# 4-MB weight units, another order of an expert's work, and the scatter as two float32r products

## The chip, the cores and the metric

One core of a Trainium2 chip runs the whole layer. The metric is the device time of one execution in microseconds (us), the median of several runs. The engines are named as the profile names them: PE is TensorE, PEld its weight loads, DVE VectorE, ACT ScalarE, POOL GpSimd, SP SyncE, which here only issues DMAs. Each engine works through its own list of instructions in the order in which the list stands.

## The reference

One post-norm decoder layer in float32 on 256 tokens of 1024 features: a mixer (a state-space branch and a gated-MLP branch), cross-attention into 256 memory tokens, and a mixture of 32 experts of which each token takes 4. The change lies in the experts:

```python
def expert_step(acc, p):
    wgu, bgu, wd, bd, g = p
    hgu = xt @ wgu + bgu
    gate = jnp.minimum(hgu[:, :D_EXPERT], SWIGLU_LIMIT)
    up = jnp.clip(hgu[:, D_EXPERT:], -SWIGLU_LIMIT, SWIGLU_LIMIT)
    glu = gate * jax.nn.sigmoid(SWIGLU_ALPHA * gate)
    y = ((up + 1.0) * glu) @ wd + bd
    return acc + g[:, None] * y.astype(f32), None
```

`g` holds a token's four softmax gates and zeros for the other experts. An expert's `w_gu` is 1024 x 2048 (8 MB), its `w_down` 1024 x 1024 (4 MB), so the experts read 384 MB, each byte once.

## The kernel before

**Phase A** (layer norm, mixer, attention, router) ends at about 392 us. It is not touched but for the names of some buffers. Towards its end SP already loads the first 22 MB of expert weights, in 1-MB pieces, into buffers that phase A leaves (`FIRST`).

**The experts** follow, two at a time as a pair (`Pair`). For a pair a 0/1 matrix picks at most 64 tokens per expert. For one expert:

- gather: products of the tokens with the 0/1 matrix (`gather`, L971), the result scaled on ACT and DVE;
- gate and up: 8 steps k of `products(k)` (L1037), each four products that stream 512 columns of weights, and then four bias products (L1044);
- SwiGLU on DVE and ACT, `gc`, `sg`, `uc` (L1049 to L1053), each instruction behind the one before;
- `hidden_t`: four transposes of `uc` on PE (L1062) and a copy on ACT (`hT`, L1063);
- down: 16 products (L1076) into `y`, which both experts of a pair share;
- after the odd expert the scatter (L1079 to L1092): ACT copies `y` to `ys` in three pieces, PE multiplies `ys` by `PT`, the transposed 0/1 matrix times the gates, in four float32 products, and DVE adds the four results to `acc`.

A float32 product of 512 columns shows as two rows in the trace, a float32r product as one. The list of PE is made by a scheduler from the order in which the program is written, and its result can differ from that order. In the program the first `AHEAD` = 2 steps of the next expert are written between the bias products and the transposes of this one.

**The weights** come in one DMA queue, issued by SP in the order of use. After `FIRST` they go round a ring of 20 MB of buffers, as ten units of 2 MB (`RING`); a unit can be issued once PE has read what lay in its place. `PT` of the next pair is made between the gathers (`weights`, L984). In expert 16 `add_rest` adds the residual and the bias of `w_down` (`b_down`, loaded in two DMAs into buffers that it shares with `ys`); it has small products with operands of 32 rows (`norm_row`, L937).

**The end**: the last pair has a form of its own. Expert 31 does its gate and up before expert 30's down; expert 30's down comes as 1-MB pieces, and expert 31's down as four column pieces of 1 MB (`w_last`), each with its own products, ACT and DVE steps and scatter (`down_piece`, `scatter_piece`).

Of the kernel before, what the change touches and what calls it, by code (L numbers as in the profile page):

```python
# [8 lines left out]
F32 = mybir.dt.float32  # L9
# [40 lines left out]
def block_kernel(ctx: ExitStack, tc: tile.TileContext, a, out):  # L50
# [12 lines left out]
    arena = cp.tile([P, len(SLOTS), 2048], F32, name="arena")  # L63
    big = ctx.enter_context(tc.tile_pool(name="big", bufs=1))

    def two(tag, dt=F32):

        return big.tile([P, 2, 2048], dt, tag=tag, name=uniq(tag))

# [133 lines left out]
    def w_parts():  # L203
        t = two(("t01", "t23")[tcount[0] % 2], F32R).rearrange("p q (i c) -> p q i c", i=2)
        tcount[0] += 1
        return [[t[:, q, i] for q in range(2)] for i in range(2)]
# [155 lines left out]
    keys(2, wk2)  # L362
    xh, xl = feat("xhl")
    for k2 in range(4):
# [330 lines left out]
    proj_residual(hh, hl, x0, x1, st)  # L695
    xh, xl = feat("xhl")
    bg3 = bgs[:96, :].bitcast(BF16)
# [255 lines left out]
    class Pair:  # L953
# [39 lines left out]
    def expert_w(src, apart=False):  # L993

        i = ucount[0]
        ucount[0] += 1
        if 2 * i < len(FIRST):
            t = []
            for h in range(2):
                name = FIRST[2 * i + h]  # L1000
                with tc.issue_after(wload[PHASE_A.index(FIRST_AFTER.get(name, ("wo", 3)))].ins):
                    if name in SLOTS:
                        t.append(bt(name))
                    elif name == "d":
                        t.append(cd[:, 1])
                    else:
                        if h == 0:
                            both = two(name)
                        t.append(both[:, h])
                    nc.sync.dma_start(t[h], src[:, h])  # L1010
            return t
        name = RING[(i - len(FIRST) // 2) % len(RING)]
        if name in SLOTS:
            at = SLOTS.index(name)
            t = arena[:, at:at + 2, :]
        else:
            t = two(name)
        if apart:
            for h in range(2):
                nc.sync.dma_start(t[:, h], src[:, h])  # L1020
        else:
            nc.sync.dma_start(t, src)
        return [t[:, h] for h in range(2)]
# [41 lines left out]

    def down(src, odd, hT, y, apart=False, between=None):

        for u in range(2):
            if u and between is not None:
                between()  # L1070
            w = expert_w(src(u), apart)
            for b in range(4):
                k = 4 * u + b
                for n in range(2):
                    o = 64 * (n ^ odd)
                    te.matmul(y[n][o:o + 64, :], hT[:, b, 64 * u:64 * u + 64],  # L1076
                              w[b // 2][:, b % 2 * D + n * 512:b % 2 * D + (n + 1) * 512], start=(k == 0), stop=(k == KB - 1))

    def scatter(y, PT, first=False):  # L1079
        ys = [wk.tile([P, 512], F32, tag="ux", name=uniq("ys")) for n in range(2)]  # L1080
        se.activation(ys[0], y[0], AF.Copy)  # L1081
        se.activation(ys[1][0:64, :], y[1][64:128, :], AF.Copy)
        se.activation(ys[1][64:128, :], y[1][0:64, :], AF.Copy)
        for n in range(2):
            for c in range(2):
                ps = pst("sm", 2)
                te.matmul(ps, PT[:, c, :], ys[n], start=True, stop=True)  # L1087
                av = acc[:, c, n * 512:(n + 1) * 512]
                if first:
# [44 lines left out]

    AHEAD = 2
    st = stats_tile(4)
# [4 lines left out]
    def before(e, k):  # L1141
# [12 lines left out]
        if e % 2 and k == 5:  # L1154
            p.weights()

    def begin(e):
        xg = pairs[e // 2].xg
        current[e] = gate_up(lambda u: a["w_gu"][e, u], i96[:, e:e + 1], lambda k: xg[:, k, e % 2 * CAP:(e % 2 + 1) * CAP],
                             lambda k: before(e, k), e == NE - 1)  # L1160

    begin(0)
    for k in range(AHEAD):
        current[0][0](k)
    for e in range(NE - 2):
# [23 lines left out]
    for k in range(AHEAD, KB):  # L1189
        current[ea][0](k)  # L1190
    uc = current[ea][1]()
    begin(eb)
    for k in range(AHEAD):
        current[eb][0](k)
    hT = hidden_t(uc)
    for k in range(AHEAD, KB):
# [8 lines left out]
    PT = pairs[ea // 2].PT  # L1205
    for q in range(4):
        if q % 2 == 0:
            w = expert_w(a["w_last"][q // 2], True)
        down_piece(hTb[0], w[q % 2], q, ys)
        if q:  # L1210
# [6 lines left out]
    with tc.For_i(0, nx, 1):  # L1217
# [35 lines left out]
        hT = hidden_t(swiglu())  # L1253
        down(lambda u: a["w_down"][bass.ds(ev, 1), u].rearrange("e p h d -> p (e h) d"), 0, hT, y)
        ys = wk.tile([P, 512], F32, tag="ux", name="ysx")
# [11 lines left out]
        for i in range(2):  # L1267
# [8 lines left out]

FIRST = ["e1", "k", "g", "gb", "xhl", "xhl", "w3", "w4", "e0", "x0", "ab", "ab", "w5", "w0", "w1", "w2", "t01", "t01", "t23",
         "t23", "j", "d"]
SLOTS = ["e1", "k", "g", "gb", "w3", "w4", "e0", "x0", "w5", "w0", "w1", "w2", "j", "h"]
FIRST_AFTER = {"e1": ("z", 1), "k": ("wq", 0), "g": ("wq", 1), "gb": ("wo", 0)}  # L1280

RING = FIRST[0:20:2]

# [15 lines left out]
def arrange(inputs):  # L1299
# [56 lines left out]
```

## Time and profile before

| | us |
|---|---|
| median of 3 runs (lowest, highest) | 1319.06 (1317.76, 1319.45) |
| the profiled execution | 1316.82 |
| its span (first to last instruction) | 1315.1 |
| phase A | 0 to 391.85 |
| experts, to the first column piece of `w_last` | 391.85 to 1288.5 |
| column pieces, last norm, output | 1288.5 to 1315.1 |

Over the span PE is busy 95%, DVE 34%, ACT 24%. The mean granted clock of PE is 0.988 of full speed. 464.4 MB of weights and inputs went through SP's queue. The profile's idle time of an engine is put down to what ended it; idle time of an engine that nobody waits for costs nothing.

### The profile page before, as it was taken

How to read it: one execution, taken by the hardware profiler on the slowest of the kernel's cores; microseconds unless marked ns; L12 is line 12 of the kernel's file. 1: busy time of each engine (PE TensorE's matmuls, PEld its weight loads, DVE VectorE, ACT ScalarE, POOL GpSimd, SP SyncE). 2: the span in 40 equal slices, each digit the busy share in tenths (PEclk: the TensorE clock that was granted, in tenths of full speed). 3: DMA queues.
4: the chain of work that ended last, by engine and by line, in shares of the span. 5: the costliest groups of instructions: out<-in, count | busy, mean ns of one | idle time of the engine just before them, and what ended most of it. 6: DMA issues, size and time to landing. Idle time of an engine off the chain costs nothing.

```text
span 1315.1 us, 15885 instructions
## 1 busy us (share of the span) xinstructions
PE 1250.8 (95%) x6757; PEld 684.9 (52%) x6758; DVE 450.3 (34%) x791; ACT 315.5 (24%) x536; POOL 29.1 (2%) x49
## 2 busy tenths in 40 slices
PE   6999999999999999999999999999999999989895
PEld 6899899989873443343333433333343433323232
DVE  4569766687441212121221112232221212212124
ACT  4746665444531111111111111101110111101000
POOL 2110000001000000000000000000000000000000
PEclk9999999999999999999999999969999999999998
DMA  9655543586788999999999999999999999999993
GB/s 357 239 176 196 192 161 133 184 290 227 275 322 353 425 426 427 427 427 428 429 428 427 428 428 427 412 428 427 427 428 428 427 428 427 428 427 427 428 424 160
DMA packets 43930, 472.00 MB, mean 359 GB/s; under 512 B 5104, under 2 KB 6928, under 8 KB 10064
## 3 DMA queue, kind: packets, MB, share of 16 engines
q1 hardware_dynamic: 39840, 464.41, 85.9%
q10 hardware_dynamic: 4016, 6.55, 1.6%
q8 instruction: 54, 0.88, 0.3%
q14 instruction: 20, 0.16, 0.0%
HBM read 469.49 MB, written 1.05 MB: 358 GB/s over the span
## 4 chain that ended last, share of the span: by engine, by line
PE 75%; DMA 18%; DVE 3%; ACT 2%; issue 1%; POOL 1%; ACTq 0%; DVEq 0%; SPq 0%; POOLq 0%
PE gu L1037 25%; PE y L1076 14%; DMA t<-in_w_gu_dram 6%; PE mm L255 6%; PE mm L239 5%; PE mm L238 5%; PE mm L237 5%; PE sm L971 4%; PE sm L1087 3%; DMA arena<-in_w_down_dram 3%; DMA ab<-in_w_gu_dram 3%; DMA arena<-in_w_gu_dram 3%; DMA t<-in_w_down_dram 2%; PE sm L1062 1%; DVE t L181 1%
## 5 line engine op out<-in xcount | busy, mean ns | idle before, releaser
L1037 PE MATMUL gu<-arena,cd 128*64 128x512 f32 x1240 | 279.8, 594 | 4.8 <-DMA arena<-in_w_gu_dram 4.8
L1037 PEld LDWEIGHTS gu<-arena,cd 128*64 128x64 f32 x1240 | 86.6, 137 | 171.5 <-issue 157.1
L181 DVE TENSOR_TENSOR t<-arena,t 128x1024 fp32r<-128x1024 f32 (+1 forms) x111 | 131.9, 1210 | 49.6 <-ACT t L180 49.6
L1076 PE MATMUL y<-arena,hT 128*64 128x512 f32 x592 | 140.7, 616 | 6.8 <-ACT hT L1063 5.6
L180 ACT ACTIVATE t<-arena 128x1024 fp32r<-128x1024 f32 (+1 forms) x114 | 113.8, 1038 | 59.2 <-PE mm L255 19.1
L1049 DVE TENSOR_SCALAR gc<-gu 128x512 f32<-128x512 f32 x32 | 22.1, 692 | 297.9 <-PE gu L1044 297.9
L237 PE MATMUL mm<-xhl,t 128*128 128x256 f32 x384 | 110.5, 288 | 0.0
L239 PE MATMUL mm<-xhl,t 128*128 128x256 f32 x384 | 108.8, 283 | 1.7 <-DVE t L181 1.7
L238 PE MATMUL mm<-xhl,t 128*128 128x256 f32 x384 | 108.7, 283 | 0.0
L1050 ACT ACTIVATE sg<-gc 128x512 f32<-128x512 f32 x32 | 20.2, 630 | 342.1 <-DVE gc L1049 342.1
L975 DVE TENSOR_SCALAR cd<-sm,par 128x128 f32<-128x128 f32 x64 | 26.2, 410 | 210.7 <-ACT cd L973 210.5
L1092 DVE TENSOR_TENSOR cd<-sm,cd 128x512 f32<-128x512 f32 x56 | 38.7, 692 | 169.3 <-PE sm L1087 169.3
L1076 PEld LDWEIGHTS y<-arena,hT 128*64 128x64 f32 x592 | 42.6, 140 | 85.9 <-issue 74.7
L1037 PE MATMUL gu<-t,cd 128*64 128x512 f32 x384 | 87.1, 595 | 0.1
L973 ACT ACTIVATE cd<-sm,par 128x128 f32<-128x128 f32 x64 | 29.3, 457 | 227.4 <-PE sm L971 226.0
L971 PEld LDWEIGHTS sm<-pair,arena 128*128 128x128 f32 x512 | 62.0, 191 | 31.7 <-issue 27.2
L239 PEld LDWEIGHTS mm<-xhl,t 128*128 128x128 f32 x384 | 73.5, 191 | 1.9 <-DVE t L181 1.9
L971 PE MATMUL sm<-pair,arena 128*128 128x128 f32 x512 | 71.3, 285 | 3.2 <-ACT pair L989 1.8
L238 PEld LDWEIGHTS mm<-xhl,t 128*128 128x128 f32 x384 | 73.6, 192 | 0.2
L237 PEld LDWEIGHTS mm<-xhl,t 128*128 128x128 f32 x384 | 73.5, 191 | 0.2
L1087 PE MATMUL sm<-ys,pair 128*128 128x512 f32 x120 | 59.1, 615 | 10.4 <-ACT ys L1081 10.2
L1037 PEld LDWEIGHTS gu<-t,cd 128*64 128x64 f32 x384 | 26.5, 137 | 50.3 <-issue 48.3
(314 smaller groups left out, 1447.8 us busy)
## 6 DMA issues: line engine op xcount, KB each, us to landing
arena<-in_w_gu_dram SPq DMA_DIRECT2D x71, 2048.0 KB, 31.8
arena<-in_w_down_dram SPq DMA_DIRECT2D x35, 2048.0 KB, 30.0
arena<-in_wa_dram SPq DMA_DIRECT2D x56, 1024.0 KB, 5.1
t<-in_w_gu_dram SPq DMA_DIRECT2D x22, 2048.0 KB, 33.8
ab<-in_w_gu_dram SPq DMA_DIRECT2D x13, 2048.0 KB, 30.1
xhl<-in_w_gu_dram SPq DMA_DIRECT2D x12, 2048.0 KB, 29.5
t<-in_w_down_dram SPq DMA_DIRECT2D x12, 2048.0 KB, 30.9
arena<-in_w_gu_dram SPq DMA_DIRECT2D x13, 1024.0 KB, 7.3
```

Of the source, the lines that this page charges most:

```text
L180: se.activation(h, src, AF.Copy)
L181: sub_op[0] = (eng or ve).tensor_tensor(l, src, h.bitcast(F32), ALU.subtract)
L237: te.matmul(ps[:, b, :], wh, xh[:, k, :], start=(k == 0), stop=False)
L238: te.matmul(ps[:, b, :], wh, xl[:, k, :], start=False, stop=False)
L239: te.matmul(ps[:, b, :], wl, xh[:, k, :], start=False, stop=(k == KB - 1))
L255: last[0] = te.matmul(res[c], x[:, k, c * P:(c + 1) * P], w[k // 2 % 2][:, k % 2, :], start=(k == 0 and i == 0), stop=(k == KB - 1 and i = ...
L971: te.matmul(pg[:, b, :], x2[:, c, k * P:(k + 1) * P], self.t[:, 0, c, :], start=(c == 0), stop=(c == 1))
L973: se.activation(self.xg[:, k, :], pg[:, 0, :], AF.Identity, bias=b2[:, k:k + 1], scale=g2[:, k:k + 1])
L1037: te.matmul(t[64 * j:64 * j + 64, :], xe(k), ws[k][:, n * D + j * 512:n * D + (j + 1) * 512], start=(k == 0), stop=False)
L1076: te.matmul(y[n][o:o + 64, :], hT[:, b, 64 * u:64 * u + 64], w[b // 2][:, b % 2 * D + n * 512:b % 2 * D + (n + 1) * 512], start=(k == 0), ...
L1087: te.matmul(ps, PT[:, c, :], ys[n], start=True, stop=True)
L1092: ve.tensor_tensor(av, ps, av, ALU.add)
```

## The change

- **Units.** The weights are laid out in HBM so that half of `w_gu` (4 MB), or the whole of `w_down`, is one block. The ring is five groups of four 1-MB slots (`RING = [8, 0, 12, 4, 16]`). Experts 0 to 3 still load in units of 2 MB, later ones in 4 MB; the last half of expert 31's `w_gu` and expert 30's `w_down` in units of 2 MB, `w_last` in 1 MB as before. Former pairs of buffers (`xhl`, `ab`, `t01`, `t23`) are now parts of two tiles of four slots.
- **Order.** `AHEAD` is 4. Written order: steps 4 to 7 of this expert, bias, SwiGLU, steps 0 to 2 of the next expert, transposes, step 3, down.
- **Scatter**, all pairs but the last. ACT's copy that makes `PT` also sums each row, which is the gate of that slot; DVE compares `PT` with 0 and gets a 0/1 matrix in float32r (`to`). ACT makes `hs`, the gated `ys` rounded to float32r, and DVE `ls`, the gated `ys` less `hs`. Eight float32r products (`to` with `hs` and with `ls`) take the place of four float32 ones. They are written behind the first steps of the next expert (`go`, called in `finish_products`).
- **`b_down`** is one DMA into a free slot (`j`) that nothing else uses by then.

The diff, cut to its core:

```diff
-RING = FIRST[0:20:2]
+RING = [8, 0, 12, 4, 16]
+NRING = 4 * len(RING)
...
-        bd = [wk.tile([NE, 512], F32, tag="ux", name=uniq("bd")) for n in range(2)]
-        for n in range(2):
-            nc.sync.dma_start(bd[n], a["b_down"][:, n * 512:(n + 1) * 512])
+        t = bt("j")
+        nc.sync.dma_start(t[:NE, :D], a["b_down"])
+        bd = [t[:NE, n * 512:(n + 1) * 512] for n in range(2)]
...
-            se.activation(self.PT, pt, AF.Copy)
+            if self.p == NE // 2 - 1:
+                se.activation(self.PT, pt, AF.Copy)
+                return
+            self.gates = wk.tile([P, 2], F32, tag="smx", name=uniq("gt"))
+            se.activation(self.PT, pt, AF.Copy, accum_out=self.gates[:, 0:1])
+            self.to = [wk.tile([P, P], F32R, tag="cbm", name=uniq("to")) for c in range(2)]
+            for c in range(2):
+                ve.tensor_scalar(self.to[c], self.PT[:, c, :], 0.0, None, op0=ALU.is_gt)
...
-            if k % 2 == 0:
-                ws[k], ws[k + 1] = expert_w(src(k // 2), last and k == KB - 2)
+            if k % 4 == 0:
+                ws.update(enumerate(expert_w(src(k // 4), n_rows[k // 4]), k))
...
-    def scatter(y, PT, first=False):
+    def scatter(y, pair, first):
+
         ys = [wk.tile([P, 512], F32, tag="ux", name=uniq("ys")) for n in range(2)]
         se.activation(ys[0], y[0], AF.Copy)
+        se.activation(ys[1][64:128, :], y[1][0:64, :], AF.Copy)
         se.activation(ys[1][0:64, :], y[1][64:128, :], AF.Copy)
-        se.activation(ys[1][64:128, :], y[1][0:64, :], AF.Copy)
+
+        hs, ls = ([wk.tile([P, 512], F32R, tag=t, name=uniq("s" + t)) for n in range(2)] for t in ("lm", "t2"))
+        g = pair.gates[:, 0:1]
         for n in range(2):
-            for c in range(2):
-                ps = pst("sm", 2)
-                te.matmul(ps, PT[:, c, :], ys[n], start=True, stop=True)
...
+            se.activation(hs[n], ys[n], AF.Copy, scale=g)
+            ve.scalar_tensor_tensor(ls[n], ys[n], g, hs[n].bitcast(F32), ALU.mult, ALU.subtract)
+
+        def go():
+            for n in range(2):
+                for c in range(2):
+                    ps = pst("sm", 2)
+                    te.matmul(ps, pair.to[c], hs[n], start=True, stop=False)
+                    te.matmul(ps, pair.to[c], ls[n], start=False, stop=True)
...
+        return go
...
-    AHEAD = 2
+    AHEAD = 4
...
+    def rows_of(e):
+
+        return (2, 2) if e < 4 else (4, 4)
...
+    def finish_products(e):
+
         products, swiglu = current.pop(e)
         for k in range(AHEAD, KB):
             products(k)
-        uc = swiglu()
+            if ready:
+                ready.pop()()
+        return swiglu()
+
+    for e in range(NE - 2):
+        uc = finish_products(e)
         begin(e + 1)
-        for k in range(AHEAD):
+        for k in range(AHEAD - 1):
             current[e + 1][0](k)
         hT = hidden_t(uc)
+        current[e + 1][0](AHEAD - 1)
...
-        down(lambda u: a["w_down"][e, u], b, hT, y)
+        down(a["w_down"][e], b, hT, y, rows_of(e)[0])
...
-            scatter(y, pairs.pop(e // 2).PT, e == 1)
+            ready.append(scatter(y, pairs.pop(e // 2), e == 1))
...
-    down(lambda u: a["w_down"][ea, u], 0, hT, y, True, lambda: hTb.append(hidden_t(uc)))
+    down(a["w_down"][ea], 0, hT, y, 2, lambda: hTb.append(hidden_t(uc)))
```

What the scheduler makes of it is read from the lists of the two programs.

PE before, from the last bias product of the odd expert 11 (`gu_4949`) to its first down product; `gu_5062` and `gu_5063` are the gate and up of expert 12:

```order
L1044 LDWEIGHTS i_109
L1044 MATMUL gu_4949<-bgs,i_109 64x512
L1037 MATMUL gu_5062<-t_35_5064,cd_3791 64x512 x2
L1037 MATMUL gu_5063<-t_35_5064,cd_3791 64x512 x2
L1037 MATMUL gu_5062<-t_35_5064,cd_3791 64x512 x2
L1037 MATMUL gu_5063<-t_35_5064,cd_3791 64x512 x2
L1062 MATMUL sm_5075<-ident,uc_5056 128x128 x4
L1076 MATMUL y_6_4973<-arena,hT_5074 64x512
```

PE of the changed kernel at the same place (`gu_4931` is expert 11's up, `gu_5044` and `gu_5045` expert 12's gate and up):

```order
L1063 LDWEIGHTS i_109
L1063 MATMUL gu_4931<-bgs,i_109 64x512
L1081 MATMUL sm_5060<-ident,uc_5038 128x128 x4
L1056 MATMUL gu_5044<-arena,cd_3731 64x512 x2
L1056 MATMUL gu_5045<-arena,cd_3731 64x512 x2
```

The next expert's products stood between the bias and the transposes, two steps of them, and now stand behind the transposes, four steps, ahead of down. It is so for the odd experts from 5 to 29 and for 4 and 30, 15 in all. For the 12 even experts from 6 to 28, eight gather products stand between bias and transposes, and on DVE the scaling of the first gather's result (a 128x128 instruction) stands ahead of `uc`'s last step. Experts 0 to 3 still have 12 products of the next expert there.

PE before at the end of expert 11's down, the last two down products and the scatter:

```order
L1076 MATMUL y_6_4973<-arena,hT_5074 64x512
L1076 MATMUL y_6_4974<-arena,hT_5074 64x512
L1087 MATMUL sm_5104<-ys_5099,pair_4708 128x512
L1087 MATMUL sm_5107<-ys_5099,pair_4708 128x512
L1087 MATMUL sm_5110<-ys_5100,pair_4708 128x512
L1087 MATMUL sm_5113<-ys_5100,pair_4708 128x512
L1037 MATMUL gu_5062<-xhl_5116,cd_3791 64x512 x2
```

PE of the changed kernel there; `slm` is `hs`, `st` is `ls`:

```order
L1093 MATMUL y_6_4970<-arena,hT_5059 64x512
L1093 MATMUL y_6_4971<-arena,hT_5059 64x512
L1113 MATMUL sm_5105<-slm_5092,to_5009 128x512
L1113 MATMUL sm_5109<-slm_5092,to_5010 128x512
L1114 MATMUL sm_5105<-st_11_5094,to_5009 128x512
L1114 MATMUL sm_5109<-st_11_5094,to_5010 128x512
L1113 MATMUL sm_5113<-slm_5093,to_5009 128x512
L1114 MATMUL sm_5113<-st_12_5095,to_5009 128x512
L1056 MATMUL gu_5044<-four_2_3788,cd_3731 64x512 x2
L1056 MATMUL gu_5045<-four_2_3788,cd_3731 64x512 x2
L1113 MATMUL sm_5117<-slm_5093,to_5010 128x512
L1114 MATMUL sm_5117<-st_12_5095,to_5010 128x512
```

Written behind step 4 of the next expert, six of the eight products stand right behind down, as the four before did. It is so for 14 pairs; in the first pair they stand among expert 2's products.

DVE of the changed kernel at this place (`uc_5038` is expert 11's; `sm_5105` to `sm_5117` are the scatter's results):

```order
L1072 SCALAR_TENSOR_TENSOR uc_5038<-uc_5038,gc_5036 128x512
L1107 SCALAR_TENSOR_TENSOR st_11_5094<-ys_5087,gt_5007,slm_5092 128x512
L1119 TENSOR_TENSOR cd_3731<-sm_5105,cd_3731 128x512
L1107 SCALAR_TENSOR_TENSOR st_12_5095<-ys_5088,gt_5007,slm_5093 128x512
L1119 TENSOR_TENSOR cd_3731<-sm_5109,cd_3731 128x512
L1119 TENSOR_TENSOR cd_3731<-sm_5113,cd_3731 128x512
L1119 TENSOR_TENSOR cd_3731<-sm_5117,cd_3731 128x512
```

Before, the four adds stood there alone; the second `ls` now stands behind the first add. On ACT the order is now: first `ys`, first `hs`, the two pieces of the second `ys`, second `hs`.

## Rows read from the trace of the kernel before

**Rows 1.** Windows: us, busy us per engine (PE, PEld, DVE, ACT, POOL), clock, DMA

```profile
391.85:1099.00 707.15, 687.17 (x3241) 267.89 (x3243) 146.08 (x295) 85.27 (x160) 0.00 (x0) 0.99 1.00 423
1099.00:1288.50 189.50, 173.11 (x806) 61.99 (x802) 33.39 (x60) 19.61 (x36) 0.00 (x0) 1.00 1.01 427
```

**Rows 2.** Waits of PE from 391.85 to 1288.5: in total, times, longest

```profile
PE sm L1087 <- ACT ys L1081: 10.2, 15, 0.7
PE y L1076 <- ACT hT L1063: 9.8, 14, 0.7
PE gu L1037 <- DMA arena<-in_w_gu_dram: 4.8, 6, 1.2
...
PE sm L1062 <- DVE uc L1053: 0.9, 1, 0.9
...
PE y L1076 <- DMA ab<-in_w_down_dram: 0.2, 1, 0.2
```

**Rows 3.** Timeline of PE, experts 2 and 3; start, us, [idle before it]

```profile
454.00 3.22 PE L1037 MATMUL gu<-xhl,cd 128*64 128x512 f32 x13
...
491.25 0.60 PE L1044 MATMUL gu<-bgs,i 96*64 96x512 bf16 x4
491.68 3.60 PE L1037 MATMUL gu<-arena,cd 128*64 128x512 f32 x16
495.22 0.66 PE L1062 MATMUL sm<-ident,uc 128*128 128x128 f32 x4
496.56 3.65 PE L1076 MATMUL y<-xhl,hT 128*64 128x512 f32 x16 [0.69 <-ACT hT L1063]
...
504.33 3.96 PE L1087 MATMUL sm<-ys,pair 128*128 128x512 f32 x8 [0.68 <-ACT ys L1081]
508.21 1.08 PE L1037 MATMUL gu<-arena,cd 128*64 128x512 f32 x4
```

**Rows 4.** Timeline of expert 31's bias products, SwiGLU and transposes

```profile
1277.75 0.60 PE L1044 MATMUL gu<-bgs,i 96*64 96x512 bf16 x4
...
1278.18 0.69 DVE L1049 TENSOR_SCALAR gc<-gu 128x512 f32<-128x512 f32 x1 [14.53 <-PE gu L1044]
...
1278.97 0.63 ACT L1050 ACTIVATE sg<-gc 128x512 f32<-128x512 f32 x1 [12.73 <-DVE gc L1049]
...
1279.63 0.69 DVE L1052 TENSOR_TENSOR gc<-gc,sg 128x512 f32<-128x512 f32 x1 [0.16 <-ACT sg L1050]
1280.36 0.69 DVE L1053 SCALAR_TENSOR_TENSOR uc<-uc,gc 128x512 f32<-128x512 f32 x1
...
1281.19 0.63 PE L1062 MATMUL sm<-ident,uc 128*128 128x128 f32 x4 [0.88 <-DVE uc L1053]
```

**Rows 5.** Timeline of a scatter: last down products and copies on ACT

```profile
657.99 7.09 PE L1076 MATMUL y<-t,hT 128*64 128x512 f32 x32 [0.69 <-ACT hT L1063]
...
665.11 0.60 ACT L1081 ACTIVATE ys<-y 128x512 f32<-128x512 f32 x1 [7.17 <-PE y L1076]
665.73 0.59 ACT L1082 ACTIVATE ys<-y 64x512 f32<-64x512 f32 x1
...
666.34 0.59 ACT L1083 ACTIVATE ys<-y 64x512 f32<-64x512 f32 x1
```

**Rows 6.** Groups of lines on PE, 300 to 391.85: busy, mean ns

```profile
L255 PE MATMUL mm<-t,cd 128*128 128x512 f32 x96 | 23.0, 395 | 0.3 <-DVE t L181 0.3
```

**Rows 7.** Groups of lines, 391.85 to 1288.5: gather products, scaling on DVE

```profile
L971 PE MATMUL sm<-pair,arena 128*128 128x128 f32 x512 | 71.3, 285 | 3.2 <-ACT pair L989 1.8 <-DVE pair L963 0.7 <-ACT hT L1063 0.6
...
L975 DVE TENSOR_SCALAR cd<-sm,par 128x128 f32<-128x128 f32 x64 | 26.2, 410 | 210.7 <-ACT cd L973 210.5
```

**Rows 8.** Windows behind `add_rest`'s small products

```profile
852.00:856.00 4.00, 2.94 (x21) 2.18 (x19) 2.78 (x7) 0.60 (x1) 0.00 (x0) 1.00 0.99 422
860.00:876.00 16.00, 16.00 (x40) 6.07 (x38) 5.40 (x9) 0.00 (x0) 0.00 (x0) 0.50 1.01 425
```

**Rows 9.** Window of 1-MB loads

```profile
1268.00:1288.00 20.00, 17.19 (x80) 5.26 (x76) 2.97 (x5) 1.48 (x3) 0.00 (x0) 1.00 1.01 420
```

More of the change, by code (lines that the diff above doesn't have):

```diff
@@ L64, in block_kernel, with fours @@
     big = ctx.enter_context(tc.tile_pool(name="big", bufs=1))
+    four = {}
+    def fours(i, dt):
+        if (i, dt) not in four:
+            four[i, dt] = big.tile([P, 4, 2048], dt, tag=f"four{i}", name=uniq(f"four{i}"))
+        return four[i, dt]
     def two(tag, dt=F32):
-        return big.tile([P, 2, 2048], dt, tag=tag, name=uniq(tag))
+        if tag == "cd":
+            return big.tile([P, 2, 2048], dt, tag=tag, name=uniq(tag))
+        at = SLOTS_R.index(tag)
+        return fours(at // 4, dt)[:, at % 4:at % 4 + 2, :]
     def bt(tag, shape=(P, 2048)):
@@ L203, in w_parts @@
     def w_parts():
-        t = two(("t01", "t23")[tcount[0] % 2], F32R).rearrange("p q (i c) -> p q i c", i=2)
+        t = two(("t0", "t2")[tcount[0] % 2], F32R).rearrange("p q (i c) -> p q i c", i=2)
         tcount[0] += 1
@@ L362, in block_kernel @@
     keys(2, wk2)
-    xh, xl = feat("xhl")
+    xh, xl = feat("xh")
     for k2 in range(4):
@@ L384, in block_kernel @@
     gbm = bt("g").rearrange("p (g d) -> p g d", g=2)
-    gvu = two("ab")
-    gv = gvu[:, 0].rearrange("p (c d) -> p c d", c=2)
+    gv = bt("h").rearrange("p (c d) -> p c d", c=2)
     st = stats_tile(2)
@@ L988, in weights @@
                 te.transpose(pt[:, c, :], G[:, c].rearrange("p b s -> p (b s)"), ident)
-            se.activation(self.PT, pt, AF.Copy)
-    ucount = [0]
[L993 to L1023, printed above, removed]
@@ new lines, in block_kernel, with slots, expert_w @@
+    ucount = [0]
+    rcount = [0]
+    def slots(i, n):
+        if i < len(SLOTS_R):
+            return fours(i // 4, F32)[:, i % 4:i % 4 + n, :]
+        i -= len(SLOTS_R)
+        return arena[:, i:i + n, :]
+    def expert_w(src, n=1):
+        out = []
+        h = src.shape[1]
+        while len(out) < h:
+            i = ucount[0]
+            if i < len(FIRST):
+                m, name = 1, FIRST[i]
+                if name == "d":
+                    t = cd[:, 1:2]
+                else:
+                    t = slots((SLOTS_R + SLOTS).index(name), 1)
+                after = tc.issue_after(wload[PHASE_A.index(FIRST_AFTER.get(name, ("wo", 3)))].ins)
+            else:
+                m = min(n, h - len(out))
+                at = (rcount[0] + NRING - len(FIRST) % 4) % NRING
+                assert at % m == 0
+                rcount[0] += m
+                t = slots(RING[at // 4] + at % 4, m)
+                after = ExitStack()
+            ucount[0] += m
+            with after:
+                nc.sync.dma_start(t, src[:, len(out):len(out) + m])
+            out += [t[:, q] for q in range(m)]
+        return out
@@ L1027, in gate_up @@
+    def gate_up(src, sel, xe, before=None, n_rows=(4, 4)):
         gp, up = pst("gu", 4), pst("gu", 4)
@@ L1064, in hidden_t, with down @@
         return hT
-    def down(src, odd, hT, y, apart=False, between=None):
-        for u in range(2):
-            if u and between is not None:
+    def down(src, odd, hT, y, rows=4, between=None):
+        w = expert_w(src, rows)
+        for k in range(KB):
+            if k == 4 and between is not None:
                 between()
[L1071 to L1077, printed above, removed]
@@ L1079, in scatter @@
-    def scatter(y, PT, first=False):
+            for n in range(2):
+                o = 64 * (n ^ odd)
+                te.matmul(y[n][o:o + 64, :], hT[:, k % 4, 64 * (k // 4):64 * (k // 4) + 64],
+                          w[k // 2][:, k % 2 * D + n * 512:k % 2 * D + (n + 1) * 512], start=(k == 0), stop=(k == KB - 1))
+    def scatter(y, pair, first):
         ys = [wk.tile([P, 512], F32, tag="ux", name=uniq("ys")) for n in range(2)]
         se.activation(ys[0], y[0], AF.Copy)
+        se.activation(ys[1][64:128, :], y[1][0:64, :], AF.Copy)
@@ new lines, in go @@
+        def go():
+            for n in range(2):
+                for c in range(2):
+                    ps = pst("sm", 2)
+                    te.matmul(ps, pair.to[c], hs[n], start=True, stop=False)
+                    te.matmul(ps, pair.to[c], ls[n], start=False, stop=True)
+                    av = acc[:, c, n * 512:(n + 1) * 512]
+                    if first:
+                        ve.tensor_copy(av, ps)
+                    else:
+                        ve.tensor_tensor(av, ps, av, ALU.add)
@@ L1159, in begin @@
         current[e] = gate_up(lambda u: a["w_gu"][e, u], i96[:, e:e + 1], lambda k: xg[:, k, e % 2 * CAP:(e % 2 + 1) * CAP],
-                             lambda k: before(e, k), e == NE - 1)
+                             lambda k: before(e, k), (4, 2) if e == NE - 1 else rows_of(e))
     begin(0)
@@ L1164, in block_kernel @@
         current[0][0](k)
-    for e in range(NE - 2):
+    ready = []
+    def finish_products(e):
         products, swiglu = current.pop(e)
@@ L1186, in block_kernel @@
                 acc = cd[:, 1].rearrange("p (c d) -> p c d", c=2)
-            scatter(y, pairs.pop(e // 2).PT, e == 1)
+            ready.append(scatter(y, pairs.pop(e // 2), e == 1))
     ea, eb = NE - 2, NE - 1
-    for k in range(AHEAD, KB):
-        current[ea][0](k)
-    uc = current[ea][1]()
+    uc = finish_products(ea)
     begin(eb)
-    for k in range(AHEAD):
+    for k in range(AHEAD - 1):
         current[eb][0](k)
     hT = hidden_t(uc)
-    for k in range(AHEAD, KB):
+    for k in range(AHEAD - 1, KB):
         current[eb][0](k)
@@ L1205, in block_kernel @@
     PT = pairs[ea // 2].PT
+    w = expert_w(a["w_last"])
     for q in range(4):
-        if q % 2 == 0:
-            w = expert_w(a["w_last"][q // 2], True)
-        down_piece(hTb[0], w[q % 2], q, ys)
+        down_piece(hTb[0], w[q], q, ys)
         if q:
@@ L1253, in block_kernel @@
         hT = hidden_t(swiglu())
-        down(lambda u: a["w_down"][bass.ds(ev, 1), u].rearrange("e p h d -> p (e h) d"), 0, hT, y)
+        down(a["w_down"][bass.ds(ev, 1)].rearrange("e p h d -> p (e h) d"), 0, hT, y)
         ys = wk.tile([P, 512], F32, tag="ux", name="ysx")
@@ L1330, in arrange @@
     wg, wd = I["w_gu"][0], I["w_down"][0]
-    r["w_gu"] = wg.reshape(NE, 4, 2, P, 2 * D).transpose(0, 1, 3, 2, 4)
-    r["w_down"] = wd.reshape(NE, 2, 4, P, D).transpose(0, 1, 3, 2, 4).reshape(NE, 2, P, 2, 2 * D)
-    r["w_last"] = wd[NE - 1].reshape(KB, P, 4, 256).transpose(2, 1, 0, 3).reshape(2, 2, P, 2 * D).transpose(0, 2, 1, 3)
+    r["w_gu"] = wg.reshape(NE, 2, 4, P, 2 * D).transpose(0, 1, 3, 2, 4)
+    r["w_down"] = wd.reshape(NE, KB, P, D).transpose(0, 2, 1, 3).reshape(NE, P, 4, 2 * D)
+    r["w_last"] = wd[NE - 1].reshape(KB, P, 4, 256).transpose(1, 2, 0, 3).reshape(P, 4, 2 * D)
     r["b_gu"], r["b_down"] = I["b_gu"][0], I["b_down"][0]
```

22 lines of the change are left out of this document (8 added, 14 removed).

## The prediction

> **What bounds the kernel now.** I read the windows of the expert phase first, then PE's waits, then the timelines of PE, DVE and ACT where the change reorders them. The windows show two kinds of bound at once [rows 1]. The DMA engines are busy throughout (last columns: share 1.00 and 1.01, 423 and 427 GB/s). PE is busy too: up to 1099 us it is idle for 707.15 - 687.17 = 20.0 us, behind that for 189.50 - 173.11 = 16.4 us. The reader is to see how the 36.4 us divide. PE's waits for a DMA are five rows, 4.8 us the longest and 0.2 us the last, 10.4 us in sum [rows 2], and they lie behind 1099. Before that nothing on PE waits for weights; it waits for ACT, 10.2 us at the scatter and 9.8 us at down. So PE sets the pace for most of the phase: it enters it behind, with 22 MB of weights already there, and the transfers run ahead by up to the ring's 20 MB. A pair of experts takes PE 508.21 - 454.00 = 54.2 us [rows 3], its 25.17 MB take the DMA engines 25.17 / 0.427 = 58.9 us. PE gains 4.7 us in a pair, and only after some twelve pairs has it caught up. The kernel is within 10.4 us of being bound by PE alone, so what PE gets to wait for or to do beyond that is paid in full, while a faster transfer is paid only as long as PE can follow.
>
> **The change, part by part.** All terms are PE's time from 391.85 to 1288.5 us. It is an account that closes: busy time plus named waits.
>
> *Transposes behind the bias.* Before, the transposes stood behind two steps of the next expert and began without a wait: bias at 491.25, products at 491.68, transposes at 495.22 with nothing idle ahead of them [rows 3]. Now they follow the bias at once in 15 experts. How long SwiGLU takes shows where it was nearly uncovered, at expert 31: the bias products end at 1277.75 + 0.60 = 1278.35, then come 0.69 us on DVE, 0.63 on ACT, 0.69 and 0.69 on DVE, and the transposes start at 1281.19 [rows 4]. That is 2.84 us, and 15 x 2.84 = 42.6. In the 12 even experts eight gather products, sixteen rows of the trace, cover 16 x 71.3 / 512 = 2.2 us of it [rows 7], but one scaling of 0.41 us now stands ahead of `uc`'s last step on DVE: 2.84 + 0.41 - 2.23 = 1.02, and 12 x 1.02 = 12.2. Together +54.8 us. From below, without that scaling's delay, 12 x 0.61, so 50; from above 55 and a little, as each restart of PE costs something. What is queued behind the waiting transposes is the whole of PE's list, and with it the release of the ring's slots. What goes: down now has four steps of products between it and its transposes, so its wait for `hT` (0.69 in the row of 496.56) is covered, -9.8; expert 31's transposes come behind eight down products, 3.5 us, -0.9.
>
> *Scatter.* Work: four float32 products take 508.21 - 504.33 = 3.88 us [rows 3]. A float32r product of 512 columns takes 23.0 / 96 = 0.24 us in phase A [rows 6], eight take 1.92. 15 x 1.96 = -29.4. Waits: the old one was for the first copy of `y`, 0.68 us each, -10.2 in all [rows 2]. The new chain from down's end at 657.99 + 7.09 = 665.08: first `ys` ready at +0.63 (665.11 + 0.60) [rows 5], first `hs`, a copy of the same size on the same engine, at +1.25, first product at +1.30, wait 1.30. Two products, 0.48; first `ls` on DVE (0.69, as `uc`'s last step of the same shape) ready at +2.03, wait 0.25. Two products to +2.51; ACT meanwhile does the two pieces of `ys` (0.59 each) and the second `hs`, ready at +3.13, wait 0.62. One product; the second `ls` stands on DVE behind the first add and is ready at +3.88, wait 0.51. The last two products stand behind four others and wait for nothing. That is 2.7 us in a pair; in the 14 pairs where they stand so, +37.5. Nearest rows from both sides: 1.25 us, which two ACT copies in a row need at least, 14 x 1.25 = 17.5; and up to 3.2 us, if the adds get in the way more often, 45. I take 37.5, since each link of the chain has a row.
>
> *Units of 4 MB.* 1-MB loads run at 420 GB/s [rows 9], 2-MB ones at 427: 2 x 2.497 - 4.911 = 0.08 us that a load costs beside its bytes. 84 pairs of loads become one, 84 x 0.083 = -7.0 us of DMA time. It is worth the 10.4 us of PE's waits at most, and with PE later than the transfers those go anyway: -10.4. No row has 4-MB loads. At the 420 GB/s of the 1-MB ones a unit would take 9.99 us rather than 9.82, and the 81 of them 14 us more in all: the transfers would still end ahead of a PE that ends 32 us later, so the term stays; at any faster rate it stays too. SP's order of loads is the old one (second half of `w_gu`, first half of the next, `w_down`), but a unit now needs four slots free instead of two. It is issued up to two steps later, some 3.5 us [rows 3], and the ring's lead covers that.
>
> *Without cost.* `b_down` no longer waits for the buffers of `ys`; only SP waited, and nothing on PE behind it. The added work on DVE and ACT (two `ls`, two `hs`, two comparisons a pair) falls on engines that were busy 146 and 85 of 707 us [rows 1]; where they are on PE's path it is counted above. The last down unit of expert 30 is 2 MB and lands as one, which leaves four more products behind its landing; with all weights there in time this is nothing, else 1.8 us. Phase A keeps its products; a few us either way belong to the range.
>
> *Sum:* 54.8 - 9.8 - 0.9 + 37.5 - 10.2 - 29.4 - 10.4 = +31.6. On the profiled execution's 1316.82 (span 1315.1) that is 1348.4. The median of the runs is 2.2 above it, so 1351. By the lower bounds, 50 - 10.7 + 17.5 - 10.2 - 29.4 - 14 (DMA waits, if each also cost a slow restart) = +3; by the upper ones, 56 and 45, +40. That is 1322 to 1359.
>
> *PE's clock.* The granted clock fell once in the phase. In 852 to 856 PE was busy 2.94 of 4 us, with products on 32 rows, and behind that, 860 to 876, the clock was 0.50, the lower level (1.2 GHz), though PE never paused [rows 8]. Those 16 us cost 8, about 10 with the edges (my estimate). I keep this fall in the sum, since `add_rest`'s products remain. The Trainium skill ("TensorE: Matmul & The Clock Gate", section "HAM oscillation — how this bites in real kernels") speaks against the change: idle gaps between groups of products let the clock fall, and each return is paid anew. By it the 2.84 us gaps might bring falls of their own, the third rival; by the row alone, where no gap was that long, there are none.
>
> **The rivals.**
>
> 1. *The transfers stay the bound, so PE's waits cost nothing.* The end of the phase goes by the DMA queue, full at 427 GB/s; PE would need 54.2 - 1.4 - 2.0 + 2.8 + 1.0 + 2.7 = 57.3 us for a pair, still under 58.9. Then the merged loads' -7.0 and the last unit's +1.8 give -5.2: 1311.6, 1314 as a median. For it: both numbers, and that PE waited for weights at the end. Against: PE gains only 1.6 us in a pair instead of 4.7, over 14 pairs 22 instead of 66, and it needed twelve pairs at 4.7 to catch up. It decides once the new waits are under 92.3 - 31.6 - 5.2 = 55 us rather than 92. At 61 there is no change.
> 2. *No clock fall at `add_rest`.* Its small products stand between others now. -10: 1341, still slower. Against: the same products, and nearly as close.
> 3. *More falls of the clock*, behind waits of 2.8 us, where PE does less in 4 us than it did in 852 to 856. +10 for each: 1361 with one, 1381 with three. Against: those products had 32 rows, the new gaps lie between full ones.
> 4. *The scatter's chain is mostly covered*, only its first two copies being seen: 17.5 instead of 37.5, so +11.6, 1331. Against: six of the eight products stand ahead of any other work of PE.
>
> **How the numbers follow.** My forecast 1351 (own range 1341 to 1360) 0.52; rival 1 0.13, at 1314; rival 2 0.15; rival 3 0.12; rival 4 0.08. The likeliest gives 1351. From below, rival 1 is left out (0.13), and from above rival 3 with two or more falls (0.06): 1320 to 1373. Within 0.2%, 2.6 us, counts as the same, which is about what a measurement of this kernel tells from no change. Rival 1 is faster but for its upper edge (0.12 and 0.01); the lower edges of rivals 4 and 2 may be the same (0.04); the rest is slower: faster 0.12, same 0.05, slower 0.83.
>
> **What would show it.** PE waits for DVE's `uc` at the transposes: 27 times, 55 us in sum, 2.8 the longest. At the scatter PE waits for ACT and DVE, some 37 us in sum. Its waits for a DMA are gone, and SP waits for PE to the end of the ring. Eight scatter products take 1.9 us. The transfers end over 10 us ahead of the first column piece, which begins near 1320. The forecast is wrong if PE still waits for weights behind 1200, if the transposes' waits are under 2 us, or if the clock takes part otherwise than once, behind `add_rest`.

## The result, and the profile after

| | before | changed |
|---|---|---|
| median, us (lowest, highest) | 1319.15 (1317.76, 1319.45), 4 runs | 1376.52 (1376.06, 1378.82), 4 runs |
| the profiled execution, its span | 1316.82, 1315.1 | 1378.82, 1377.1 |
| ratio to before | | 1.0445, 95% interval 1.0433 to 1.0458 |
| mean granted clock | 0.988 | 0.964 |

The change makes the kernel slower, as forecast, but by 57 us instead of 32, and outside the range. The chain that ended last holds no DMA any more, where it was 18% before:

```profile
PE 87%; DVE 8%; ACT 3%; issue 1%; DMA 0%; ACTq 0%; DVEq 0%
```

The waits of PE in the expert phase, 387 to 1345 us (in total, times, longest), against [rows 2]:

```profile
PE sm L1081 <- DVE uc L1072: 52.9, 27, 2.8
PE sm L1113 <- ACT slm L1106: 20.2, 14, 1.4
PE sm L1113 <- DVE cd L1119: 9.0, 14, 0.6
```

No wait for a DMA is left, and none for `hT`. The wait at the transposes is there 27 times, as counted from the order. The timeline of expert 11 shows one of the 15 long ones, from the bias products to the next expert's first ones (start, us, engine, what; idle before it in brackets), against [rows 3, 4]:

```profile
724.51 0.60 PE L1063 MATMUL gu<-bgs,i 96*64 96x512 bf16 x4
...
724.94 0.69 DVE L1068 TENSOR_SCALAR gc<-gu 128x512 f32<-128x512 f32 x1 [13.20 <-PE gu L1063]
...
725.72 0.63 ACT L1069 ACTIVATE sg<-gc 128x512 f32<-128x512 f32 x1 [14.43 <-DVE gc L1068]
726.38 0.69 DVE L1071 TENSOR_TENSOR gc<-gc,sg 128x512 f32<-128x512 f32 x1 [0.16 <-ACT sg L1069]
727.11 0.69 DVE L1072 SCALAR_TENSOR_TENSOR uc<-uc,gc 128x512 f32<-128x512 f32 x1
...
727.86 1.11 PE L1081 MATMUL sm<-ident,uc 128*128 128x128 f32 x4 [2.74 <-DVE uc L1072]
...
728.90 8.11 PE L1056 MATMUL gu<-arena,cd 128*64 128x512 f32 x32
```

The reader is to see two things. The chain of DVE and ACT is the one of expert 31 before, and PE idles 2.74 us for it. And the four transposes take 1.11 us, where they took 0.63 [rows 4]. The windows tell why (us, busy us of PE, PEld, DVE, ACT, POOL, clock, DMA share, GB/s), against [rows 1, 8]:

```profile
387.20:1353.80 966.60, 875.80 (x4045) 336.65 (x4045) 202.62 (x415) 127.42 (x241) 0.00 (x0) 0.95 0.94 396
724.50:727.60 3.10, 0.61 (x6) 0.12 (x2) 2.47 (x4) 0.63 (x1) 0.00 (x0) 1.00 0.98 423
727.60:731.00 3.40, 3.14 (x10) 1.49 (x12) 0.20 (x1) 0.60 (x1) 0.00 (x0) 0.50 0.96 414
731.00:735.00 4.00, 4.00 (x20) 1.26 (x18) 0.00 (x0) 0.00 (x0) 0.00 (x0) 1.00 1.04 451
744.00:748.10 4.10, 1.96 (x6) 0.80 (x6) 2.21 (x4) 3.14 (x5) 0.00 (x0) 1.00 0.98 424
748.10:751.50 3.40, 3.40 (x9) 1.04 (x9) 1.22 (x2) 0.00 (x0) 0.00 (x0) 0.50 1.03 443
898.30:915.40 17.10, 16.83 (x38) 6.50 (x38) 6.76 (x11) 0.00 (x0) 0.00 (x0) 0.50 0.43 184
```

In 724.5 to 727.6 PE works 0.61 of 3.1 us, at full clock; right behind it the granted clock is 0.50, the lower of the two levels (1.2 GHz), for 3.4 us, and from 731 it is 1.00 again. Behind the scatter of the same expert (744 to 748.1, PE busy 1.96 of 4.1 us) there is another such fall. Over the phase the clock record has 22 of them, 92.2 us at half speed, against one of 20.5 us before. All 15 long waits at transposes have a fall behind them, 5 of the 14 scatters, and two other stretches of small products one each, the one behind `add_rest` 17.1 us long. None of the 12 short waits at transposes (1 us) has one. The Trainium skill ("TensorE: Matmul & The Clock Gate", section "HAM oscillation — how this bites in real kernels") describes the pattern: idle gaps between groups of products let the clock fall, and each return is paid anew. The trace agrees in that, with 15 of 15. The gaps of the page's example are longer waits, for DMAs; here gaps of 2.74 us came before a fall, and the measurement decides.

The scatter of expert 11, from the first copy of `y` on, against [rows 5]:

```profile
743.91 0.60 ACT L1099 ACTIVATE ys<-y 128x512 f32<-128x512 f32 x1 [14.31 <-PE y L1093]
744.54 0.72 ACT L1106 ACTIVATE slm<-ys,gt 128x512 fp32r<-128x512 f32 x1
...
745.30 0.75 DVE L1107 SCALAR_TENSOR_TENSOR st<-ys,gt,slm 128x512 fp32r<-128x512 f32 x1 [17.50 <-ACT slm L1106]
...
745.32 0.73 PE L1113 MATMUL sm<-slm,to 128*128 128x512 f32 x2 [1.44 <-ACT slm L1106]
...
746.10 0.73 PE L1114 MATMUL sm<-st,to 128*128 128x512 f32 x2
746.52 0.72 ACT L1106 ACTIVATE slm<-ys,gt 128x512 fp32r<-128x512 f32 x1
746.64 0.69 DVE L1119 TENSOR_TENSOR cd<-sm,cd 128x512 f32<-128x512 f32 x1 [0.59 <-PE sm L1114]
747.27 0.75 DVE L1107 SCALAR_TENSOR_TENSOR st<-ys,gt,slm 128x512 fp32r<-128x512 f32 x1
...
747.48 0.47 PE L1113 MATMUL sm<-slm,to 128*128 128x512 f32 x1 [0.64 <-DVE cd L1119]
```

PE waits 1.44 us for the first `hs`, and 0.64 before the fifth product, for the first add to give its buffer back. The two engines' instructions that write float32r take 0.72 (ACT) and 0.75 us (DVE). Two products take 0.73, one 0.47. Over the phase (busy us, mean ns, idle before), the old scatter first and then the two lines of the new one:

```profile
L1087 PE MATMUL sm<-ys,pair 128*128 128x512 f32 x120 | 59.1, 615 | 10.4 <-ACT ys L1081 10.2
...
L1114 PE MATMUL sm<-st,to 128*128 128x512 f32 x60 | 25.7, 466 | 2.7
L1113 PE MATMUL sm<-slm,to 128*128 128x512 f32 x60 | 25.6, 465 | 29.2 <-ACT slm L1106 20.2 <-DVE cd L1119 9.0
```

### The profile page after: what moved, and what is told of

Its sections match the earlier page's. It is cut to its first block, busy times and chain, and to the rows that moved or that the text cites. A ratio compares the mean times of both kernels' runs of the same rounds, so it can differ in the third digit from the quotient of the medians.

```text
span 1377.1 us, 15899 instructions
## 1 busy us (share of the span) xinstructions
PE 1263.7 (92%) x6758; PEld 692.3 (50%) x6758; DVE 473.9 (34%) x851; ACT 344.8 (25%) x581; POOL 29.5 (2%) x49
## 4 chain that ended last, share of the span: by engine, by line
PE 87%; DVE 8%; ACT 3%; issue 1%; DMA 0%; ACTq 0%; DVEq 0%
PE gu L1056 35%; PE y L1093 16%; PE mm L265 8%; PE mm L248 5%; PE mm L249 5%; PE mm L247 5%; PE sm L980 3%; PE sm L1081 2%; DVE st L1107 2%; PE sm L1114 1%; DVE gc L1068 1%; DVE gc L1071 1%; DVE uc L1072 1%; ACT sg L1069 1%; ACT slm L1106 1%; DVE cd L1119 1%
## 5 line engine op out<-in xcount | busy, mean ns | idle before, releaser
L1056 PE MATMUL gu<-arena,cd 128*64 128x512 f32 x1240 | 292.9, 622 | 0.0
L1056 PE MATMUL gu<-four,cd 128*64 128x512 f32 x800 | 194.5, 635 | 0.0
L191 DVE TENSOR_TENSOR four<-arena,four 128x1024 fp32r<-128x1024 f32 (+1 forms) x119 | 137.8, 1168 | 83.2 <-ACT four L190 75.8
L190 ACT ACTIVATE four<-arena 128x1024 fp32r<-128x1024 f32 (+1 forms) x122 | 122.1, 1014 | 103.1 <-PE mm L248 49.0
L247 PE MATMUL mm<-four,four 128*128 128x256 f32 x496 | 142.2, 287 | 0.0
L248 PE MATMUL mm<-four,four 128*128 128x256 f32 x496 | 140.5, 283 | 0.0
L249 PE MATMUL mm<-four,four 128*128 128x256 f32 x496 | 140.5, 283 | 0.0
L1093 PE MATMUL y<-arena,hT 128*64 128x512 f32 x576 | 133.4, 609 | 0.0
L1056 PEld LDWEIGHTS gu<-four,cd 128*64 128x64 f32 x800 | 58.4, 145 | 115.3 <-issue 114.1
L1107 DVE SCALAR_TENSOR_TENSOR st<-ys,gt,slm 128x512 fp32r<-128x512 f32 x30 | 22.5, 752 | 257.8 <-ACT slm L1106 257.8
L247 PEld LDWEIGHTS mm<-four,four 128*128 128x128 f32 x496 | 95.1, 192 | 0.2
L248 PEld LDWEIGHTS mm<-four,four 128*128 128x128 f32 x496 | 95.1, 192 | 0.2
L249 PEld LDWEIGHTS mm<-four,four 128*128 128x128 f32 x496 | 95.0, 192 | 0.0
L1093 PE MATMUL y<-four,hT 128*64 128x512 f32 x416 | 91.9, 593 | 0.0
```

The source lines that it names most:

```text
L190: se.activation(h, src, AF.Copy)
L191: sub_op[0] = (eng or ve).tensor_tensor(l, src, h.bitcast(F32), ALU.subtract)
L247: te.matmul(ps[:, b, :], wh, xh[:, k, :], start=(k == 0), stop=False)
L248: te.matmul(ps[:, b, :], wh, xl[:, k, :], start=False, stop=False)
L249: te.matmul(ps[:, b, :], wl, xh[:, k, :], start=False, stop=(k == KB - 1))
L1093: te.matmul(y[n][o:o + 64, :], hT[:, k % 4, 64 * (k // 4):64 * (k // 4) + 64], w[k // 2][:, k % 2 * D + n * 512:k % 2 * D + (n + 1) * 512] ...
```

## The experiments

The first theory: PE is the bound, and what it waits for at transposes and scatters, with the falls of the clock behind these waits, is the whole loss. Rivals: the 4-MB transfers are slow or have gaps (their rate over the phase is down to 396 GB/s); the scatter is the larger part; the clock falls for another reason than the gaps. Ratios are to the kernel before; where one is below 1, the difference is under 1% and the interval leaves 1 out.

**Transposes covered.** The changed kernel, the transposes ordered behind three steps of the next expert (an extract; `products` now returns its last product, and expert 30 has the same order):

```diff
...
         for k in range(AHEAD - 1):
-            current[e + 1][0](k)
-        hT = hidden_t(uc)
+            step = current[e + 1][0](k)
+        with tc.issue_after(step.ins):
+            hT = hidden_t(uc)
...
```

Expected:

> The changed kernel with one thing undone: the transposes of each expert are ordered behind three steps of the next expert's products, as the program has them written; scatter, 4-MB units and the rest stay. Theory A (PE is the bound; its waits at the transposes, 52.9 us, and the clock falls that follow them, some 16 of 3.4 us at half speed, 1.7 us each, make the loss): PE's own sum falls by 53 + 27 to about 1297 and the transfers become the bound, 1312 to 1322. Theory B (the transfers of 4 MB are slower or have gaps, 395 GB/s over the phase): stays at 1370 or more. Theory C (the scatter's chain is the larger part of the loss): about 1350.

Measured: 1310.33 us (1309.32 to 1312.17), ratio to before 0.9948 (0.9933 to 0.9964). That single order takes off 66 us and ends below the kernel before. Its waits of PE in the phase:

```profile
PE sm L1114 <- ACT slm L1107: 20.1, 14, 1.4
PE sm L1114 <- DVE cd L1120: 9.0, 14, 0.6
PE sm L980 <- ACT pair L1003: 7.6, 11, 0.7
PE y L1094 <- DMA four<-in_w_down_dram: 1.5, 1, 1.5
```

The wait for `uc` is gone, the scatter's stay as they were, one for weights has come, and there are 7 clock falls, 44 us at half speed. Theory B is out: the transfers did not set the time of the changed kernel. Theory C is out as well. Theory A's cause holds, but not its end: PE waits only 1.5 us for weights, so the transfers are not the bound here. PE still sets the pace, with the falls that are left and a longer wait for `pair` at the gathers (7.6 us; 2.5 in the changed kernel).

**Scatter late.** The changed kernel, `go()` called behind step 6 and ordered there (an extract):

```diff
...
-            products(k)
-            if ready:
-                ready.pop()()
+            step = products(k)
+            if ready and k == 6:
+                with tc.issue_after(step.ins):
+                    ready.pop()()
...
```

Expected:

> The changed kernel with the scatter's products ordered behind step 6 of the next expert; the transposes stay behind the bias (the first of the four in odd experts, all four in even ones). Theory A: the scatter's waits of 29.2 us go, and the five clock falls that came behind a scatter, 5 x 1.7; 1376 - 38 = 1338, with the transposes' 53 us still there and a clock fall behind each. Theory B: 1370 or more. Theory C: under 1325.

Measured: 1344.34 us (1343.12 to 1348.26), ratio 1.0199 (1.0183 to 1.0214). The scatter's waits and the falls behind it go, and the transposes' wait stays:

```profile
PE sm L1082 <- DVE uc L1073: 50.2, 26, 2.8
PE sm L980 <- ACT pair L1003: 8.2, 12, 0.7
```

It takes off 32 us, six less than theory A's 38. Time at half speed goes from 92.2 to 78.5 us, half of the difference is 6.8 instead of 8.5, and PE's wait for `pair` at the gathers rises from 2.5 to 8.2 us.

**Both.** Both edits. Expected:

> The changed kernel with both undone: transposes behind three steps of the next expert, scatter's products behind step 6. Theory A: PE's sum would be 1376 - 53 - 29 - 37 = 1257, so the transfers bound it: 1319.1 less 7 for the merged loads and 1.5 for the bias load, plus 2 for the last unit, 1312 to 1315; the clock falls at most at the small products of expert 16; PE waits for DMA some 50 us. Theory B: 1365 or more. If 4-MB loads bring nothing: 1317 to 1320.

Measured: 1309.34 us (1307.64 to 1309.84), ratio 0.9934 (0.9921 to 0.9948). It beats both kernels, and ends 3 us below what the theory gave. PE's waits are now mainly for weights, 31 us in four rows, where the theory had some 50:

```profile
PE gu L1056 <- DMA arena<-in_w_gu_dram: 12.8, 8, 2.5
PE gu L1056 <- DMA four<-in_w_gu_dram: 8.3, 5, 2.5
...
PE y L1094 <- DMA arena<-in_w_down_dram: 5.9, 3, 2.0
PE y L1094 <- DMA four<-in_w_down_dram: 4.0, 2, 2.0
```

and the transfers run at (same columns as above):

```profile
1100.00:1250.00 150.00, 133.07 (x636) 50.17 (x634) 27.70 (x52) 20.19 (x37) 0.00 (x0) 1.00 1.01 432
```

The theory allowed one fall of the clock, behind expert 16's small products; there are five, 30.7 us at half speed. Against the kernel with only the transposes covered, 1310.33 us, the late scatter changes nothing beyond the runs: now the transfers are the bound.

**The gap filled.** The changed kernel with products added in the long gaps, so that PE works through them (an extract):

```diff
...
+        if fill is not None:
+            with tc.issue_after(fill.ins):
+                for i in range(12):
+                    te.matmul(pt, onesB, onesB[:, 0:1].to_broadcast([P, 512]), start=True, stop=True)
...
```

`fill` is the last bias product of the 15 experts, `pt` the block that the transposes overwrite. Expected:

> The changed kernel with 12 bf16 products of 512 columns added between bias and transposes of the 15 experts in which these stand together; their result is overwritten by the transposes. The waits are not shortened, PE works through them. If gaps on PE bring the clock falls (theory A): the 15 falls behind the transposes go, 15 x 1.7 and the longer first one, so 1376 - 27 = 1349 (1345 to 1356), and the falls behind scatters stay. If the falls come from something else (the float32r products, the load as such): 1376 as before.

Measured: 1355.97 us (1352.36 to 1364.72), ratio 1.0281 (1.0264 to 1.0298), at the upper edge of theory A's range. Expert 11 again, and below it the window from its transposes on (columns as above), where the clock stays at 1.00:

```profile
722.09 0.60 PE L1064 MATMUL gu<-bgs,i 96*64 96x512 bf16 x4
...
722.63 2.78 PE L1084 MATMUL sm<-onesB 128*128 128x512 bf16 x12
...
724.69 0.69 DVE L1073 SCALAR_TENSOR_TENSOR uc<-uc,gc 128x512 f32<-128x512 f32 x1
...
725.44 0.66 PE L1087 MATMUL sm<-ident,uc 128*128 128x128 f32 x4
```

```profile
725.40:729.00 3.60, 3.57 (x19) 1.48 (x20) 0.00 (x0) 0.60 (x1) 0.00 (x0) 1.00 1.01 437
```

Bias to transposes is still 3.35 us, as in the changed kernel: nothing was shortened. But the transposes take 0.66 us again, and in the profiled execution none of the 15 places has a clock fall behind it; the falls behind scatters rose from 5 to 9, and three lie at other small products. Time at half speed went from 92.2 to 64.9 us, half of the difference is 13.7 us, and the profiled executions differ by 1378.82 - 1364.72 = 14.1. So the gaps bring these falls, and what a fall costs is about half its length. The median lies 21 us lower than that of the changed kernel. The profiled run is the slowest of the four: its mean granted clock is 0.973, that of the other three 0.979 to 0.981, so the others had less time at half speed. That is worth some 9 us (an estimate, 0.007 of 1355 us), about their distance from it.

**2-MB units.** The changed kernel with `return (2, 2)` in `rows_of`. Expected:

> The changed kernel with 2-MB units throughout (one constant changed); order as written, scatter and bias load stay. The scheduler then leaves eight products of the next expert between bias and transposes, in odd and even experts, except for expert 30. Theory A1 (the 4-MB units alone moved the transposes): their waits and the falls behind them go, PE's sum is 1376 - 50 - 27 = 1299, and the 2-MB transfers bound the time, 1316 to 1321. Theory A2 (the new order of work or the scatter costs as much by itself): above 1340.

Measured: 1314.83 us (1313.78 to 1315.71), ratio 0.9973 (0.9962 to 0.9984), 1 us below theory A1's range. The order of work and the scatter are as written in the changed kernel, and yet:

```profile
PE sm L1113 <- ACT slm L1106: 20.1, 14, 1.4
...
PE y L1093 <- DMA arena<-in_w_down_dram: 5.5, 5, 1.3
...
PE sm L1081 <- DVE uc L1072: 2.7, 1, 2.7
```

One wait at transposes is left, expert 30's. So it was the size of the units that moved the transposes: with 2-MB units the scheduler keeps two steps of the next expert ahead of them, with 4-MB units it does not. Why is not in any trace.

**Before, transposes behind the bias.** The converse, in 13 experts of the kernel before (an extract; `tr[0]` is the last transpose, the other experts keep their order):

```diff
...
+        if e % 2 and e > 4:
+            hT = hidden_t(uc)
+            with tc.issue_after(tr[0].ins):
+                for k in range(AHEAD):
+                    current[e + 1][0](k)
...
```

Expected:

> The kernel before with one thing done: in the 13 odd experts from 5 to 29 the transposes are ordered right behind the bias, and the next expert's two steps behind them. Theory A: 13 waits of 2.75 us, 13 falls of the clock at 1.7 us, less 9 us of waits for the copy of the transposed block and 10 of waits for weights: 1318 + 36 + 22 - 19 = 1357 (1345 to 1362). If the transfers hide PE's waits (rival 1 of the prediction): 1318 to 1325. If the clock falls need the float32r scatter: 1335.

Measured: 1350.92 us (1347.47 to 1352.02), ratio 1.0248 (1.0232 to 1.0264), inside theory A's range. Its waits of PE at transposes and scatters:

```profile
PE sm L1063 <- DVE uc L1054: 36.9, 14, 2.8
PE sm L1088 <- ACT ys L1082: 10.2, 15, 0.7
```

36.9 us of waits; 58.0 us at half speed instead of 20.5, with 10 of the 13 gaps followed by a fall (the other three are as long, 2.74 to 2.83 us), so 18.8 us; the waits for `hT` (9.1) and for weights (10.4) gone: 36.9 + 18.8 - 19.5 = +36, measured +32. No float32r scatter and no 4-MB unit is needed for it.

**Covered, 2-MB units.** Both covers, `rows_of` as above. Expected:

> The kernel with both covers (transposes behind three steps, scatter behind step 6) with 2-MB units throughout. Bound by transfers; 4-MB units ran at 431 to 432 GB/s there, 2-MB ones at 427 to 428 before, so 81 pairs of loads apart cost 7 to 9 us: 1316 to 1319. If the unit size is worth nothing to the transfers: 1309.

Measured: 1314.26 us (1313.28 to 1316.48), ratio 0.9971 (0.9961 to 0.9981), 2 us below the range.

```profile
1100.00:1250.00 150.00, 134.87 (x630) 48.60 (x628) 26.76 (x51) 18.67 (x35) 0.00 (x0) 1.00 1.01 428
```

428 GB/s against 432, and 4.9 us more than with 4 MB; the two intervals lie apart, so this is what the larger units are worth when nothing else is late. What is left of the gain over the kernel before, 4.3 us, no run takes apart. The experts' first ring load lands at 400.2 us here, at 405.2 in the kernel before; but the last weights land only 1.6 us earlier (1294.0, 1295.6), and the stretch from the first column piece on is 3.4 us shorter.

**Covered, old scatter.** 4-MB units, transposes covered, the float32 scatter of before at its old place. Expected:

> The kernel with the transposes covered and 4-MB units, but with the float32 scatter of the kernel before, at its old place behind down. PE works and waits some 19 us more than with the covered float32r scatter (59 + 10 us against 50); that kernel waits 31 us for weights, so the transfers still bound: 1309 to 1313. If the float32r scatter is what brings the gain: 1318 or more.

Measured: 1308.77 us (1306.52 to 1309.69), ratio 0.9923 (0.9909 to 0.9936).

```profile
PE sm L1105 <- ACT ys L1099: 10.2, 15, 0.7
...
PE gu L1056 <- DMA arena<-in_w_gu_dram: 4.0, 2, 2.2
```

The same as with the new scatter, within the runs: PE waits 10.2 us at the scatter as before, and 9.8 us for weights where the kernel with both covers waits 31.0. What the old scatter costs PE comes off its waits for weights, so here the scatter's form is worth nothing.

## Why the prediction was wrong

| term, us | forecast | profile |
|---|---|---|
| waits at transposes, less `hT` and `uc` before | 54.8 - 10.7 = +44.1 | 52.9 - 10.7 = +42.2 |
| scatter, work and waits, less those before | -29.4 + 37.5 - 10.2 = -2.1 | 51.3 + 31.9 - 59.1 - 10.4 = +13.7 |
| waits for weights | -10.4 | -10.4 |
| clock, half of 92.2 - 20.5 us | 0 | +35.8 |
| other work and waits of the phase | 0 | -11.3 |
| expert phase | +31.6 | 966.6 - 896.6 = +70.0 |
| phase A; column pieces and end | 0 | -4.7; -3.3 |
| span | +31.6 | +62.0 |

- **The bound** was read rightly: PE, with the transfers hidden behind it. The covers showed it from both sides: taking away PE's waits took 66 us, and doing them to the kernel before added 32.
- **The transposes' term** was right to 2 us; it came from the order of the instructions and one nearly uncovered chain in the trace of before.
- **The clock is the step that failed.** The sum kept the one fall of before and put new ones at nothing: "by the row alone, where no gap was that long, there are none" took the absence of long gaps in the kernel before for an absence of falls. The runs showed 22 falls instead of one and +35.8 us, nearly the whole of the 38.4 that the phase missed. The third rival had the mechanism, but with one to three falls at 10 us each, priced by the one fall before; it was 21 more falls, 20 of them of 3.4 us and so 1.7 us each. That its 1381 for three falls lies near the measured 1376.5 is luck: too few falls, at too high a price. The number of falls could have been put at the number of long gaps, 15. A clock that takes part otherwise than once was among the signs that the prediction named for being wrong.
- **The scatter's term was mis-sized** by 16 us, and by its work: 51.3 us where the forecast had 15 x 1.92 = 28.8. The 0.24 us for a float32r product holds in a long run of them; here two take 0.73 and a single one 0.47, so a pair's eight are busy 51.3 / 15 = 3.4 us instead of 1.92. Its waits came out lower than forecast, 31.9 us against 37.5, though not link by link: `hs` and `ls` take 0.72 and 0.75 us instead of the 0.60 and 0.69 put for them, which makes the first wait 1.44 us instead of 1.30, and the fifth product waits for the buffer that the first add gives back, not for the second `hs`.
- **Rival 1** (the transfers stay the bound) fell with the result, but its mechanism is that of the kernel with both covers, which waits 31 us for weights. It ends at 1309, 5 us below the rival's 1314. There the merged loads brought 4.9 us, where 81 of them at 0.083 would be 6.7. Phase A, costed at nothing, ended 4.7 us earlier in the changed kernel. The change touches more of it than names of buffers: the order in which the first weights fill the free buffers (`FIRST`) is another one too. No run separates that.
- The rest of the phase, -11.3, is settled in part. About half of it, 5.7 us, is the scatter's term counted too high: of its 51.3 us, 1.6 are what half speed added, which the clock's term holds too, and in 4.1 other products run as well. The products of down take 7.5 us less of PE's time at full clock than before (216.0 against 223.5). Why is not shown, and no run separates it.

## What to carry to other kernels

Before a change of sizes or of written order, read the order that comes out of it: here a larger load moved four small transposes in front of the work that had covered their input, and with 2-MB units, which leave them covered, the changed kernel took 1314.8 us instead of 1376.5. A wait on an engine that bounds the kernel costs its length, and on TensorE the work behind it may run at half clock; look for the longest idle gap that the change makes, and compare it with gaps whose sequel a trace shows. Where no trace shows one as long, the falls are unknown, not none. If the order is what matters, pin it: ordering the transposes alone turned a loss of 4.4% into a gain of 0.5%, and the scatter's products as well made it 0.7%.

## What the runs showed of the hardware

- Gaps of about 2.74 us between busy products were followed by a fall of the granted clock to 0.50 in 15 of 15 cases in the changed kernel and 10 of 13 in the kernel before with moved transposes, so the length of a gap does not decide it alone; most falls lasted 3.4 us. The 12 gaps of about 1 us at transposes were not. With the long gaps filled by bf16 products, 0 of 15.
- Loads of 4 MB ran at 431 to 432 GB/s where 2-MB loads ran at 427 to 428, in stretches in which the DMA engines were busy throughout.
- An ACT copy of 128x512 took 0.72 us when it read `ys` and wrote float32r with a scale from a tile, 0.60 us as a plain float32 copy of the products' result; which of the differences costs the 0.12 us is not shown.
- A float32r product of 512 columns began 0.24 to 0.34 us after the one before it in the groups of four of the kernel with both covers; alone between waits one was busy 0.47 us.
